# Streaming-encoder trunk on one core: first output sums inside the last input block, regrouped pairs, a fixed load order

## The chip, the core and the metric

One core of a Trainium2 chip runs the whole kernel. The metric is the device time of one execution in microseconds; the time before is 2336.9 us, the median of three runs (2333.71 to 2339.33). The engines are called as in the profile: PE (matrix products) with PEld (its weight loads), DVE (VectorE), ACT (ScalarE), POOL (GpSimd) and SP (SyncE, which here only issues loads).

## The reference, cut to what matters

```python
for i in range(2):
    hn = rmsnorm(h, norm_mix_g[i])
    mix = s5_mixer(hn, ...) if i == 0 else shortconv_mixer(hn, conv_w_in, conv_w, conv_w_out)
    h = h + mix
    gate, up = split(rmsnorm(h, norm_ffn_g[i]) @ ffn_w_in[i])      # 1024 -> 2 x 2816
    h = h + (silu(gate) * up) @ ffn_w_out[i]                       # 2816 -> 1024
    g = sigmoid(rmsnorm(h, norm_ple_g[i]) @ ple_w_gate[i])
    h = h + g * (p[i] @ ple_w_up[i])
return rmsnorm(h, final_norm_g)
# short convolution: b, c, v = split(u @ w_in); y = (b * conv3(c * v)) @ w_out
```

Everything is float32; the sequence has 1024 positions and the model 1024 channels.

## The kernel before, in words

**Precision.** A float32 product is made of three products of a narrower form: each operand is split into a high part (an ACT cast, L90) and a low part (a DVE subtraction, L91), and `mm3` (L123 to L126) adds high x high, high x low and low x high into one PSUM bank. `unit_of` (L118) splits a loaded raw tile into such a pair.

**Tiling.** The 1024 positions are eight row tiles of 128 (`T` = 8, `HT` = 4); tile q and tile q+4 go together as a step q. The big products use a seven-product scheme for 2 x 2 blocks (Strassen's, in a form with few sums), so that for each pair of blocks seven products and a number of sums stand in place of eight products.

**FFN input** (`ffn_in`, L441). 22 blocks, j and j+11 in turn. For each, `weights_set` (L310) loads two raw tiles, makes four sums on DVE and seven split operands in the ring `ws`; `block_product` (L340) makes seven products of 12 matmuls, each 512 wide, with ACT and DVE combining the results. The seven moving operands of a block lie in `ulow` (four of them, quarters `L0` to `L15`, sixteen) and `uhigh` (three, quarters `H0` to `H11`). The hidden units go to DRAM in seven combinations for each j (`hidden[j]`, tile `hw`), by POOL's queue (L456), five stores behind the second block of each j.

**FFN output** (`ffn_out`, L486). The 11 hidden pairs are taken in six groups, two pairs each but the last, which has one. For each group and each of the four steps q: seven products, each of three matmuls a pair, added to rows of h by DVE (`add`, L579) or by an ACT copy and a POOL add (`add_slow`, L586). The operands of a pair come from two raw weight tiles: four subtractions (L508, L512, L517, L520) and seven units, each in a quarter (`make`, L494). Rooms alternate: an even group has the first fourteen low quarters in a list, an odd one the twelve high ones and the last two low ones. The units of the first group are made at the head of `ffn_out` (`run_all(begun)`, L562), those of a later group at the end of the steps of the group before (L621). In the last group each step normalises its two tiles for the gate product (`post`, L609 and L618; `norm_tile`, L193) and the gate's first operands are made (`following`, L623, L625).

**Gate product** (`ple`, L641): for two halves of the columns, eight tiles of 24 matmuls, operands in rooms of `uhigh` and the four tiles `s8t`, which in `ffn_out` hold the chunks of hidden units.

**Convolution** (`conv_in`, `conv_out`). `conv_in` uses the same block product; `conv_out` calls `out_phase` (L382): two groups of four 128-row units, and for each of the eight tiles a chunk of the hidden tensor (`ch`, L403) and, in the first group, the row h of the tile (L406).

**Order.** A planner orders each engine's instructions ahead of time from the order of the program, its own costs and due times; `first()` moves an instruction up by 100 places. Within an engine that order is then fixed. `tc.issue_after(x)` puts what it encloses behind x on x's engine. In `ffn_out` all loads go through `queue` (L532), which chains each SP load behind the one before; `out_phase` only puts the load of h behind the chunk of the same tile. Raw tiles take four slots in turn (`raw_tile`, L95). A pool's memory is reused tile by tile: a load into a new tile waits for the last use of what lay there.

**Between the stages.** `last_pairs` (L251) turns the last rows into the moving operands while the first block already runs, through `others` (L229); the first weight set is loaded early, the second (`weights_set` without `early`) in the ordinary way.

Of the kernel before, what the change touches and what calls it, by code (L numbers as in the profile page):

```python
# [24 lines left out]
def trunk(  # L25
# [225 lines left out]
    def last_pairs(xs, gb):  # L251


        a, z = HT - 2, HT - 1
        with tc.issue_after(done["sum"]), tc.issue_after(done["square"]):
            p = {(0, 0): transposed(xs[a], 0), (1, 0): transposed(xs[a + HT], 0), (1, 1): transposed(xs[a + HT], 1),
                 (0, 1): transposed(xs[a], 1, mm)}
            put(0, a, p[0, 0])
            xs[z], xs[T - 1] = normed(z, gb, 2), normed(T - 1, gb, 2)
            r = {(0, i): transposed(xs[z], i, mm) for i in range(2)}  # L260
            put(0, z, r[0, 0])
            others(a, p)
            n = len(tc.nc.cur_bb.bb.instructions)
            r.update({(1, i): transposed(xs[T - 1], i) for i in range(2)})
            held[:] = [i for i in tc.nc.cur_bb.bb.instructions[n:] if i.engine == PE.engine]
            others(z, r)

# [42 lines left out]
    def weights_set(src_a, src_b):  # L310


        ra, rb = early.pop() if early else [load_raw(src, "p (kt n) -> p kt n", kt=KT) for src in (src_a, src_b)]
        a11, a12, a21, a22 = ra[:, 0:512], ra[:, 512:D], rb[:, 0:512], rb[:, 512:D]

        def operand(src):
            w = wsp.tile([P, 2, 512], F32R, name="ws", tag="ws")
            split(w[:, 0], w[:, 1], src)
            return w

        def s_tile():
            return stp.tile([P, 512], F32, name="st", tag="st")

        w11 = operand(a11)
        s3 = s_tile()
        V.tensor_tensor(s3, a11, a21, ALU.subtract)
        V.tensor_tensor(a21, a21, a22, ALU.add)
        s2 = s_tile()
        V.tensor_tensor(s2, a21, a11, ALU.subtract)
        ws2 = operand(s2)  # L330
        ws1 = operand(a21)
        w12 = operand(a12)
        ws3 = operand(s3)
        V.tensor_tensor(s2, a12, s2, ALU.subtract)
        return [w11, ws2, ws1, w12, ws3, operand(s2), operand(a22)]
# [4 lines left out]
    def block_product(ws, on_c11=None):  # L340


        def prod(ps, i, start):
            for kt in range(KH):
                sl = slice(kt * P, (kt + 1) * P)
                mm3(ps, ws[i][:, 0, sl], ws[i][:, 1, sl], moving(i, kt, 0), moving(i, kt, 1),
                    start and kt == 0, kt == KH - 1, more=not start)

# [33 lines left out]
    def out_phase(wout, groups, last_post, following=(), hold=True):  # L382


        def fetch(ht, room):
            return unit_of(room(), load_raw(wout[ht], "p n -> p n"))

        units = {ht: fetch(ht, room) for ht, room, _ in groups[0]}
        kept = []
        for gi, group in enumerate(groups):  # L390
# [5 lines left out]
            for t in ORDER:  # L396
                parts = {}
                for ht, *_ in group:
                    if ht // 4 not in parts:
                        parts[ht // 4] = ch = raw_tile(shape=(P, 4, 2, P), dt=F32R, name="ch")  # L400
                        of = [x[0] % 4 for x in group if x[0] // 4 == ht // 4]
                        ks = slice(min(of), max(of) + 1)
                        load = nc.sync.dma_start(out=ch[:, ks].bitcast(F32), in_=hid[ht // 4][t, :, ks])  # L403
                if gi == 0:
                    with tc.issue_after(load.ins):
                        nc.sync.dma_start(out=h[t], in_=hdram[t])  # L406
# [34 lines left out]
    def ffn_in(l):  # L441
# [7 lines left out]
        def product(ht):  # L449
            ws = weights_set(win[:, :, ht * P:(ht + 1) * P], win[:, :, HID + ht * P:HID + (ht + 1) * P])  # L450
            return block_product(ws, silu)
# [33 lines left out]

    def ffn_out(l, post, following):  # L486
        wout = ffn_w_out[l].rearrange("(ht p) n -> ht p n", p=P)
        lows = [quarter_low(i) for i in (0, 4, 8, 12, 1, 5, 9, 13, 2, 6, 10, 14, 3, 7, 11, 15)]
        highs = [quarter_high(i) for i in range(12)]
        groups = [list(range(g, min(g + 2, NK))) for g in range(0, NK, 2)]  # L490
        rooms = [lows[:14] if g % 2 == 0 else highs + lows[14:] for g in range(len(groups))]
        combo = {1: 0, 2: 2, 3: 5, 4: 6, 5: 3, 6: 4, 7: 1}

        def make(j, room, got):  # L494
            ra, rb = (raw_tile() for _ in range(2))
            for raw, i in ((ra, j), (rb, j + NK)):
                queue(raw, wout[i])
            if j in groups[0]:
                yield
            b11, b12, b21, b22 = ra[:, 0:512], ra[:, 512:D], rb[:, 0:512], rb[:, 512:D]  # L500

            def unit(i, src):
                v = room.pop(0).rearrange("p (l n) -> p l n", l=2)
                got[i] = unit_of((v[:, 0], v[:, 1]), src)

            unit(1, b11)
            yield
            V.tensor_tensor(b12, b12, b11, ALU.subtract)  # L508
            unit(5, b12)
            yield  # L510
            unit(3, b22)
            V.tensor_tensor(b22, b22, b12, ALU.subtract)  # L512
            unit(6, b22)
            yield
            unit(2, b21)
            yield
            V.tensor_tensor(b11, b22, b11, ALU.subtract)  # L517
            unit(7, b11)
            yield
            V.tensor_tensor(b21, b21, b22, ALU.subtract)  # L520
            unit(4, b21)

        def run_all(gens):
            gens = list(gens)
            while gens:
                for g in list(gens):
                    if next(g, gens) is gens:
                        gens.remove(g)

        queued = []  # L530

        def queue(to, src):  # L532
            with tc.issue_after(queued.pop()) if queued else ExitStack():
                queued.append(nc.sync.dma_start(out=to, in_=src).ins)

# [19 lines left out]
        units = {j: {} for j in range(NK)}  # L555
        begun = []
        for j in groups[0]:
            fetch(0, 0, [j])
            begun.append(make(j, rooms[0], units[j]))
            next(begun[-1])  # L560
        rows(0)
        run_all(begun)  # L562
        pending = []
        for gi, group in enumerate(groups):
            last = gi == len(groups) - 1
            todo = [] if last else [make(j, rooms[gi + 1], units[j]) for j in groups[gi + 1]]
            for q in range(HT):
# [34 lines left out]
                prod(a, 6, False)  # L602
                soft(a, 0, 1)
# [5 lines left out]
                if last:  # L609
                    post(q)  # L610
                prod(a, 7, False)
                add(a, 1, 1, True)

                def finish(a=a, prod=prod, add=add, last=last, q=q):
                    prod(a, 4, False)
                    add(a, 1, 0, True)
                    if last:
# [5 lines left out]
                elif last and following and q > 0:  # L623
                    following.pop(0)()
                if gi == len(groups) - 2 and q > 1:  # L625
                    following.pop(0)()
# [14 lines left out]
    def ple(l, units, post, ahead):  # L641
        more, makers = ple_units(l, 1, [room_new(i) for i in (1, 2, 3, 0)])
        for nb in range(2):
# [5 lines left out]
            for t in ORDER:  # L649
# [16 lines left out]
                if nb == 0 and len(makers) > 2:  # L666
# [647 lines left out]
    def ffn_ple(l, last, ahead):  # L1314
        units, makers = ple_units(l, 0, [room_high(4), room_high(5), room_new(3), room_new(0)])
# [53 lines left out]
```

## Time and profile before

| | us |
|---|---|
| median of three runs | 2336.9 |
| profiled execution, its own time | 2336.83 |
| its span | 2335.1 |
| last FFN input block of layer 0, on PE | 824.2 to 843.2 |
| FFN output of layer 0 | 847.0 to 1091.9 |
| convolution's output, PE | 1437.5 to 1546.0 |
| FFN output of layer 1 | 1987.2 to 2233.5 |

The page gives busy time by engine, the chain that ended last and the costliest groups. A busy time by stretch counts the instructions that touch the stretch, with the granted TensorE clock behind them. In the timeline, a bracket at the end of a line is the idle time of the engine just before that instruction and what ended it. `SPq` and `POOLq` are lines of a sequencer that issues loads or stores.

### The profile page before, as it was taken

To read this page: it belongs to the slowest core of one execution; us is meant where nothing else is said; L and a number is where in the kernel's file an instruction comes from. 1 tells how busy PE (TensorE), PEld (TensorE's weight loads), DVE (VectorE), ACT (ScalarE), POOL (GpSimd) and SP (SyncE) were. 2 spreads that over 40 slices of the span, in tenths; PEclk is the share of its full clock that TensorE was granted. 3 is DMA by queue.
4 is the path that set the end of the run, shared out by engine and by line. 5 is a ranking of instruction groups with operands and counts; after the bars stand their busy time and mean duration, and the time that the engine had idled before them with its cause. 6 is when DMAs were issued, how large, how long until landed. Compare 5 with 4: busy or idle time off the path is not lost.

```text
span 2335.1 us, 27847 instructions
## 1 busy us (share of the span) xinstructions
PE 2189.7 (94%) x9989; PEld 1793.4 (77%) x9989; DVE 1641.1 (70%) x2760; ACT 899.4 (39%) x1717; POOL 350.8 (15%) x426
## 2 busy tenths in 40 slices
PE   7888999899999989999979999979999999799998
PEld 5777887788888867777858887768888888677777
DVE  7885326877777768677587776387777776877674
ACT  6554223444343433234343333154444443333242
POOL 2110001011111113332010000011111111223310
PEclk8999999899999989999989999989999999899999
DMA  8555202344444466672232324433544445775613
GB/s 247 145 137 154 64 19 80 101 144 157 141 153 145 154 256 259 242 275 95 95 104 81 107 92 144 180 127 125 172 145 154 150 154 183 267 259 220 245 55 109
DMA packets 234010, 358.14 MB, mean 153 GB/s; under 512 B 23696, under 2 KB 166032, under 8 KB 233872
## 3 DMA queue, kind: packets, MB, share of 16 engines
q1 hardware_dynamic: 203040, 247.24, 32.2%
q0 software_dynamic: 30432, 109.08, 13.6%
q8 instruction: 79, 1.29, 0.2%
q14 instruction: 59, 0.48, 0.1%
q10 hardware_dynamic: 400, 0.04, 0.0%
HBM read 225.53 MB, written 114.29 MB: 146 GB/s over the span
## 4 chain that ended last, share of the span: by engine, by line
PE 38%; issue 35%; DVE 13%; DMA 7%; POOL 5%; SPq 1%; ACT 1%; POOLq 0%; DVEq 0%; ACTq 0%
PE psmm L124 12%; PE psmm L125 12%; PE psmm L126 12%; POOL hw L456 5%; DVE h L582 2%; DMA raw<-in_ffn_w_out_dram 2%; DVE ulow L91 2%; DMA tw<-tmp 1%; DVE uhigh L91 1%; DVE gv L1160 1%; DVE W L810 1%; DMA h<-hd 1%; DVE tmp L810 1%; DMA hw<-hs 1%; DVE raw L512 1%
## 5 line engine op out<-in xcount | busy, mean ns | idle before, releaser
L124 PE MATMUL psmm<-ulow,ws 128*128 128x512 f32 x896 | 353.4, 396 | 16.3 <-ACT ulow L90 13.8
L125 PE MATMUL psmm<-ulow,ws 128*128 128x512 f32 x896 | 352.7, 394 | 2.5 <-DVE ulow L91 2.5
L126 PE MATMUL psmm<-ulow,ws 128*128 128x512 f32 x896 | 352.1, 393 | 2.0 <-DVE ws L91 2.0
L124 PE MATMUL psmm<-uhigh,ws 128*128 128x512 f32 x672 | 261.8, 390 | 1.8 <-DVE u L361 1.1
L126 PE MATMUL psmm<-uhigh,ws 128*128 128x512 f32 x672 | 261.5, 389 | 0.0
L125 PE MATMUL psmm<-uhigh,ws 128*128 128x512 f32 x672 | 261.4, 389 | 0.0
L456 POOL DMA_DIRECT2D hw<-hs x154 | 116.0, 754 | 792.4 <-DVE hs L91 764.7
L582 DVE TENSOR_TENSOR h<-psmm,h 128x512 f32<-128x512 f32 x244 | 163.5, 683 | 100.4 <-PE psmm L126 57.1
L90 ACT CAST ws<-raw 128x512 fp32r<-128x512 f32 x224 | 138.3, 621 | 193.8 <-PE psmm L126 181.7
L124 PEld LDWEIGHTS psmm<-ulow,ws 128*128 128x128 f32 x896 | 170.9, 191 | 53.1 <-ACT ulow L90 14.7
L125 PEld LDWEIGHTS psmm<-ulow,ws 128*128 128x128 f32 x896 | 170.6, 190 | 39.3 <-DVE ulow L91 3.5
L126 PEld LDWEIGHTS psmm<-ulow,ws 128*128 128x128 f32 x896 | 170.5, 190 | 38.7 <-DVE ws L91 3.0
L591 POOL TENSOR_TENSOR h<-part,h 128x512 f32<-128x512 f32 x92 | 138.6, 1507 | 295.0 <-ACT part L590 225.1
L124 PE MATMUL psmm<-ulow,w 128*128 128x512 f32 x368 | 150.6, 409 | 26.6 <-DVE h L582 12.5
L91 DVE TENSOR_TENSOR ws<-raw,ws 128x512 fp32r<-128x512 f32 x224 | 152.9, 685 | 10.2 <-ACT ws L90 10.1
L125 PE MATMUL psmm<-ulow,w 128*128 128x512 f32 x368 | 148.7, 404 | 6.2 <-DVE ulow L91 6.2
L90 ACT CAST ws<-st 128x512 fp32r<-128x512 f32 x168 | 103.7, 618 | 117.7 <-PE psmm L126 107.6
L124 PEld LDWEIGHTS psmm<-uhigh,ws 128*128 128x128 f32 x672 | 126.2, 188 | 29.2 <-DVE s L369 1.5
L126 PE MATMUL psmm<-ulow,w 128*128 128x512 f32 x368 | 147.8, 402 | 0.0
L126 PEld LDWEIGHTS psmm<-uhigh,ws 128*128 128x128 f32 x672 | 126.1, 188 | 26.2
L125 PEld LDWEIGHTS psmm<-uhigh,ws 128*128 128x128 f32 x672 | 126.2, 188 | 26.1
L125 PE MATMUL psmm<-w,ulow 128*128 128x512 f32 (+1 forms) x328 | 126.2, 385 | 0.0
(267 smaller groups left out, 4442.5 us busy)
## 6 DMA issues: line engine op xcount, KB each, us to landing
hw<-hs POOLq DMA_DIRECT2D x154, 512.0 KB, 4.2
w<-hw SPq DMA_DIRECT2D x88, 768.0 KB, 5.9
raw<-in_ffn_w_in_dram SPq DMA_DIRECT2D x88, 512.0 KB, 4.0
raw<-in_ffn_w_out_dram SPq DMA_DIRECT2D x44, 512.0 KB, 7.6
hd<-h POOLq DMA_DIRECT2D x24, 512.0 KB, 3.0
h<-hd SPq DMA_DIRECT2D x24, 512.0 KB, 7.4
raw<-in_conv_w_in_dram SPq DMA_DIRECT2D x24, 512.0 KB, 3.8
w<-hw SPq DMA_DIRECT2D x88, 128.0 KB, 5.8
```

The costliest lines, as they stand in the source:

```text
L90: A.copy(hi, src)
L91: V.tensor_tensor(lo, src, hi.bitcast(F32), ALU.subtract)
L124: PE.matmul(ps, ahi, bhi, start=start, stop=False, skip_group_check=more)
L125: PE.matmul(ps, ahi, blo, start=False, stop=False, skip_group_check=more)
L126: PE.matmul(ps, alo, bhi, start=False, stop=stop, skip_group_check=more)
L456: nc.gpsimd.dma_start(out=hidden[j][:, :, c].rearrange("q p l j -> p q l j"), in_=hs.bitcast(F32))
L512: V.tensor_tensor(b22, b22, b12, ALU.subtract)
L582: done["sum"] = V.tensor_tensor(h[t][:, cs], ps, h[t][:, cs], ALU.add).ins
L591: G.tensor_tensor(h[t][:, cs], part, h[t][:, cs], ALU.add)
L810: V.tensor_tensor(o, a, b, op)
L1160: V.tensor_tensor_scan(gv[:, g, 1:P], dec, sv[:, g, 1:P], 0.0, ALU.mult, ALU.add)
```

## The change

The diff has six parts.

1. `ffn_out`'s first two pairs are begun inside the last input block: `begin` issues the four weight loads, `block_product` calls `beside(i)` behind product i, and that takes so many steps of the two makers (two each behind the products 0 and 2, one behind 3, three behind 4). The second pair's subtractions go to POOL.
2. The groups are 2, 2, 2, 1, 2, 2 pairs; each pair has a written-out list of quarters; pairs 6 and 7 are made in the third group, 8 in the fourth.
3. In the last group the tiles 2 and 6 are normalised in the last step, and the gate's makers are called two, one, none and one in its steps; the gate's rooms move by one. In a single pair's step the add to the lower right block goes the slow way.
4. `last_pairs` notes the last ACT instruction of its parts, and the second weight set's first operand is issued behind it on ACT.
5. `out_phase` chains its loads: chunk, then row, one tile ahead in the first group, and the later units' weights in the same chain.
6. `make`, `run_all` and `queue` move out of `ffn_out` unchanged but for the above.

```diff
@@ last_pairs
             others(z, r)
+            done["others"] = next(i for i in reversed(tc.nc.cur_bb.bb.instructions) if i.engine == A.engine)
@@ weights_set
+        second = not early and done.pop("others", None)
         ra, rb = early.pop() if early else [load_raw(src, "p (kt n) -> p kt n", kt=KT) for src in (src_a, src_b)]
...
-        w11 = operand(a11)
+        with tc.issue_after(second) if second else ExitStack():
+            w11 = operand(a11)
@@ block_product
-    def block_product(ws, on_c11=None):
+    def block_product(ws, on_c11=None, beside=None):
...
+            if beside:
+                beside(i)
@@ out_phase
-            return unit_of(room(), load_raw(wout[ht], "p n -> p n"))
+            raw = raw_tile()
+            if queued:
+                queue(raw, wout[ht])
+            else:
+                nc.sync.dma_start(out=raw, in_=wout[ht])
+            return unit_of(room(), raw)
+
+        queued.clear()
...
+            def chunk(t, gi=gi, group=group):
+                j = group[0][0] // 4
+                assert [x[0] for x in group] == list(range(4 * j, 4 * j + 4))
+                ch = raw_tile(shape=(P, 4, 2, P), dt=F32R, name="ch")
+                queue(ch.bitcast(F32), hid[j][t])
                 if gi == 0:
-                    with tc.issue_after(load.ins):
-                        nc.sync.dma_start(out=h[t], in_=hdram[t])
+                    queue(h[t], hdram[t])
+                return {j: ch}
+
+            if gi == 0:
+                coming = chunk(ORDER[0])
+            for n, t in enumerate(ORDER):
+                if gi:
+                    parts = chunk(t)
+                else:
+                    parts, coming = coming, None if t == ORDER[-1] else chunk(ORDER[n + 1])
@@ ffn_in
-            return block_product(ws, silu)
+            return block_product(ws, silu, begin(l) if ht == NHT - 1 else None)
@@ ahead of ffn_out
+    groups = [[0, 1], [2, 3], [4, 5], [6], [7, 8], [9, 10]]
+    ROOMS = ["L0 L8 L1 L13 L6 L3 H1", "L4 L12 L5 L2 L10 H0 H2", "L7 L9 L11 L14 L15 H3 H4", "H5 H6 H7 H8 H9 H10 H11",
+             "L0 L8 L1 L13 L6 L3 H1", "L4 L12 L5 L2 L10 H0 H2", "L9 L11 L14 L15 H3 H4 H5", "L7 H6 H7 H8 H9 H10 H11",
+             "L0 L1 L2 L3 L4 L5 L6", "L8 L10 L12 L13 H0 H1 H2", "L9 L11 L14 L15 H3 H4 H5"]
+    MADE = (1, 5, 3, 6, 2, 7, 4)
...
+    def make(l, j, got, eng=None):
+        eng = eng or V
...
+        for raw, i in ((ra, j), (rb, j + NK)):
+            queue(raw, wout[i])
+        yield
...
+        unit(1, b11)
+        yield
+        eng.tensor_tensor(b12, b12, b11, ALU.subtract)
+        unit(5, b12)
+        yield
...
+    def begin(l):
+        units.clear()
+        units.update({j: {} for j in range(NK)})
+        queued.clear()
+        gens = [make(l, j, units[j], G if j else V) for j in groups[0]]
+        for g in gens:
+            next(g)
+        steps = {0: (0, 1, 0, 1), 2: (0, 1, 0, 1), 3: (0,), 4: (1, 0, 1)}
+
+        def beside(i):
+            for g in steps.get(i, ()):
+                next(gens[g], None)
+        return beside
@@ ffn_out
-        groups = [list(range(g, min(g + 2, NK))) for g in range(0, NK, 2)]
-        rooms = [lows[:14] if g % 2 == 0 else highs + lows[14:] for g in range(len(groups))]
...
-        for j in groups[0]:
-            fetch(0, 0, [j])
-            begun.append(make(j, rooms[0], units[j]))
-            next(begun[-1])
+        fetch(0, 0)
         rows(0)
-        run_all(begun)
...
-            todo = [] if last else [make(j, rooms[gi + 1], units[j]) for j in groups[gi + 1]]
+            todo = {2: [6, 7], 3: [8]}.get(gi, [] if last else groups[gi + 1])
+            todo = [make(l, j, units[j]) for j in todo]
...
                 prod(a, 6, False)
+                if last and q == HT - 1:
+                    post(HT - 2)
+                    post(T - 2)
...
-                if last:
+                if last and q != HT - 2:
                     post(q)
                 prod(a, 7, False)
-                add(a, 1, 1, True)
+                if len(group) == 1:
+                    add_slow(a, 1, 1)
+                else:
+                    add(a, 1, 1, True)
...
-                    if last:
+                    if last and q != HT - 2:
                         post(q + HT)
...
-                elif last and following and q > 0:
-                    following.pop(0)()
-                if gi == len(groups) - 2 and q > 1:
-                    following.pop(0)()
+                if last:
+                    for _ in range((2, 1, 0, 1)[q]):
+                        following.pop(0)()
@@ ple
-        more, makers = ple_units(l, 1, [room_new(i) for i in (1, 2, 3, 0)])
+        more, makers = ple_units(l, 1, [room_new(i) for i in range(4)])
...
-                if nb == 0 and len(makers) > 2:
+                if nb == 0 and len(makers) > 1:
                     makers.pop(0)()
@@ ffn_ple
-        units, makers = ple_units(l, 0, [room_high(4), room_high(5), room_new(3), room_new(0)])
+        units, makers = ple_units(l, 0, [room_high(3), room_high(4), room_high(5), room_new(3)])
```

More of the change, by code (lines that the diff above doesn't have):

```diff
@@ L395, in out_phase @@
             soon, late = [f for early, f in todo if early], [f for early, f in todo if not early]
[L396 to L403, printed above, removed]
-                if gi == 0:
-                    with tc.issue_after(load.ins):
-                        nc.sync.dma_start(out=h[t], in_=hdram[t])
+            def chunk(t, gi=gi, group=group):
[3 more added lines that the diff above has]
+                queue(ch.bitcast(F32), hid[j][t])
+                if gi == 0:
+                    queue(h[t], hdram[t])
[7 more added lines that the diff above has]
+                    parts, coming = coming, None if t == ORDER[-1] else chunk(ORDER[n + 1])
                 ps = [psum() for _ in range(2)]
@@ L484, in quarter_high @@
         return uhigh.rearrange("p c k l j -> p (c k l j)")[:, i * D:(i + 1) * D]
-    def ffn_out(l, post, following):
-        wout = ffn_w_out[l].rearrange("(ht p) n -> ht p n", p=P)
-        lows = [quarter_low(i) for i in (0, 4, 8, 12, 1, 5, 9, 13, 2, 6, 10, 14, 3, 7, 11, 15)]
-        highs = [quarter_high(i) for i in range(12)]
-        groups = [list(range(g, min(g + 2, NK))) for g in range(0, NK, 2)]
-        rooms = [lows[:14] if g % 2 == 0 else highs + lows[14:] for g in range(len(groups))]
-        combo = {1: 0, 2: 2, 3: 5, 4: 6, 5: 3, 6: 4, 7: 1}
[L494 to L534, printed above, removed]
@@ new lines, in trunk, with queue @@
+    groups = [[0, 1], [2, 3], [4, 5], [6], [7, 8], [9, 10]]
[3 more added lines that the diff above has]
+    MADE = (1, 5, 3, 6, 2, 7, 4)
+    queued = []
+    def queue(to, src):
+        with tc.issue_after(queued.pop()) if queued else ExitStack():
+            queued.append(nc.sync.dma_start(out=to, in_=src).ins)
@@ new lines, in run_all, with unit @@
+    def run_all(gens):
+        gens = list(gens)
+        while gens:
+            for g in list(gens):
+                if next(g, gens) is gens:
+                    gens.remove(g)
+    def make(l, j, got, eng=None):
+        eng = eng or V
+        wout = ffn_w_out[l].rearrange("(ht p) n -> ht p n", p=P)
+        rooms = {i: (quarter_low if r[0] == "L" else quarter_high)(int(r[1:])) for i, r in zip(MADE, ROOMS[j].split())}
+        ra, rb = (raw_tile() for _ in range(2))
+        for raw, i in ((ra, j), (rb, j + NK)):
+            queue(raw, wout[i])
+        yield
+        b11, b12, b21, b22 = ra[:, 0:512], ra[:, 512:D], rb[:, 0:512], rb[:, 512:D]
+        def unit(i, src):
+            v = rooms[i].rearrange("p (l n) -> p l n", l=2)
+            got[i] = unit_of((v[:, 0], v[:, 1]), src)
+        unit(1, b11)
[3 more added lines that the diff above has]
+        yield
+        unit(3, b22)
+        eng.tensor_tensor(b22, b22, b12, ALU.subtract)
+        unit(6, b22)
+        yield
+        unit(2, b21)
+        yield
+        eng.tensor_tensor(b11, b22, b11, ALU.subtract)
+        unit(7, b11)
+        yield
+        eng.tensor_tensor(b21, b21, b22, ALU.subtract)
+        unit(4, b21)
@@ new lines, in trunk @@
+    units = {}
+    def begin(l):
[10 more added lines that the diff above has]
+        return beside
+    def ffn_out(l, post, following):
+        combo = {1: 0, 2: 2, 3: 5, 4: 6, 5: 3, 6: 4, 7: 1}
@@ L554, in ffn_out @@
         steps = [(gi, q) for gi in range(len(groups)) for q in range(HT)]
-        units = {j: {} for j in range(NK)}
-        begun = []
-        for j in groups[0]:
-            fetch(0, 0, [j])
-            begun.append(make(j, rooms[0], units[j]))
-            next(begun[-1])
+        fetch(0, 0)
         rows(0)
-        run_all(begun)
         pending = []
```

## The prediction

> **What bounds the kernel now.** I read the page first, then busy times by stretch of the matmul engine, then its waits, then the timeline of the stretches that lose time.
>
> ```profile
> span 2335.1 us, 27847 instructions
> ## 1 busy us (share of the span) xinstructions
> PE 2189.7 (94%) x9989; PEld 1793.4 (77%) x9989; DVE 1641.1 (70%) x2760; ACT 899.4 (39%) x1717; POOL 350.8 (15%) x426
> ```
>
> PE is the bound, so a change can win only what PE loses. The profiled execution took 2336.83 us, 1.7 more than its span, and the median of the runs is 2336.9; the sum is made against 2336.8 and stands for the median too.
>
> Busy time by stretch, all engines: one whole block of the FFN's input (the last of layer 0), then a piece of what follows it. The columns are PE, PEld, DVE, ACT, POOL with their counts, granted clock, DMA share, GB/s.
>
> ```profile
> 824.25:843.25 19.00, 18.98 (x84) 15.39 (x82) 7.29 (x11) 3.62 (x6) 1.50 (x2) 1.00 0.79 296
> 845.00:850.00 5.00, 1.25 (x2) 0.74 (x3) 4.88 (x9) 2.77 (x6) 2.84 (x4) 0.66 1.02 402
> ```
>
> 84 matmuls in 19.00 us is 0.226 us for a 512-wide one when nothing is in the way. In this block DVE is free for 19.00 - 7.29 = 11.7 us and ACT for 15.4, because no next weights are prepared; straight after it DVE is full and PE starves. The same view for PE alone, at the places that the change touches:
>
> ```profile
> 843.25:866.90 23.65, 12.11 (x27) 0.71 0.78 305
> 870.60:1061.80 191.20, 184.79 (x799) 1.00 0.69 254
> 1059.30:1091.80 32.50, 26.85 (x120) 0.95 0.26 89
> 1457.50:1467.90 10.40, 3.72 (x9) 0.67 0.94 364
> 1983.50:2007.20 23.70, 12.34 (x27) 0.71 0.79 300
> 2010.85:2203.80 192.95, 185.97 (x799) 0.99 0.68 252
> 2201.40:2233.45 32.05, 26.94 (x116) 0.89 0.25 91
> ```
>
> Start of the FFN's output, both layers: 27 matmuls are worth 27 x 0.226 = 6.1 us but took 23.65 and 23.70, so 17.5 us are lost each time, part of them because the granted clock is 0.71. The groups behind it lose 191.20 - 798 x 0.226 = 10.8 us and 12.6 (one of the 799 reaches over the edge), spread thinly. The last group: 84 matmuls (19.0 us) and 36 or 32 transposes; at 0.11 us for a transpose (the row of eight below) that is 23.0 and 22.5 against 32.50 and 32.05: 9.5 us lost each. The convolution's output: 10.40 - 9 x 0.226 = 8.4 us lost.
>
> ```profile
> 1089.60 1.03 PE L204 MATMUL pstr<-ident,xn 128*128 128x128 f32 x8
> ```
>
> What ended PE's waits:
>
> ```profile
> PE psmm L124 <- ACT ulow L90: 23.9, 7, 6.0
> PE psmm L124 <- DVE h L582: 22.5, 22, 3.4
> ```
>
> L90 on ulow is mostly the making of the first operands of the FFN's output; L582 is the adding of products to h.
>
> **Part 1: the first sums inside the last input block.** Timeline, PE, then ACT and DVE:
>
> ```profile
> 846.98 0.80 PE L124 MATMUL psmm<-ulow,w 128*128 128x512 f32 x1 [3.76 <-ACT ulow L90]
> ...
> 863.38 0.61 PE L124 MATMUL psmm<-ulow,w 128*128 128x512 f32 x1 [3.39 <-DVE h L582]
> ```
>
> ```profile
> 848.92 1.66 ACT L90 CAST ulow<-raw 128x512 fp32r<-128x512 f32 x3 [1.99 <-DVE raw L508]
> ```
>
> ```profile
> 860.24 1.89 DVE L91 TENSOR_TENSOR ulow<-raw,ulow 128x512 fp32r<-128x512 f32 x3
> 862.04 0.68 DVE L91 TENSOR_TENSOR hs<-s,hs 128x512 fp32r<-128x512 f32 x1
> 862.64 0.68 DVE L582 TENSOR_TENSOR h<-psmm,h 128x512 f32<-128x512 f32 x1
> ```
>
> After the block DVE makes 14 operands and 8 subtractions, 22 operations, and only behind them comes the first add to h (862.64), for which PE waits a second time. In a row a DVE operation costs (1.89 - 0.68)/2 = 0.605 us and an ACT cast (1.66 - 0.62)/2 = 0.52. The change moves all of it under the block's products: 14 casts = 7.3 us in ACT's 15.4 free, and on DVE 14 + 4 = 18 operations = 10.9 us in its 11.7 free; four subtractions of the second pair go to POOL, which has 17.5 free. So it just fits, and the 17.5 us go, if the weights are there:
>
> ```profile
> 828.02 0.90 SPq L534 DMA_DIRECT2D raw<-in_ffn_w_out_dram  x2
> 832.38 1.49 SPq L534 DMA_DIRECT2D w<-hw  x2
> 833.98 0.94 SPq L534 DMA_DIRECT2D raw<-in_ffn_w_out_dram  x2
> 834.97 1.26 SPq L534 DMA_DIRECT2D h<-hd  x2
> 837.82 6.24 SPq L534 DMA_DIRECT2D w<-hw  x4
> 848.35 3.09 SPq L534 DMA_DIRECT2D h<-hd  x2
> ```
>
> The second pair's weights were issued behind a hidden-unit load that waited for room until 832.38. Now the four weight loads are first in the chain and wait only for the raw slots of the last two weight sets, which are read before the block starts; they should go by about 822. The hidden loads that they pass are held by their own rooms, so they lose nothing.
>
> What is late next: (a) the block's closing work, about 8 DVE operations after its last product (4.9 us), against a first add due one product (6 x 0.226 = 1.4 us) in. PE can do one more product, so the add costs between 0 (it goes first) and 4.9 + 0.6 - 2.7 = 2.8 us; I take 2.5, since the closing work is older in the plan. (b) The rows of h for the second step:
>
> ```profile
> h<-hd SPq DMA_DIRECT2D x8, 512.0 KB, 7.8
> ```
>
> Issued at 848.35 and 851, they land at about 859. Without loss the second step starts at 843.25 + 42 x 0.226 = 852.7, its third product ends at 856.8, PE does one more to 858.2 and then needs that add, done at 859.6: 1.4 us. (c) Bytes: a step of the first group now loads two hidden sets of 917,504 bytes (the shape in the code), two rows of h and two weight rows of 524,288 each, 3.93 MB. At the 402 GB/s of the row above that is 9.8 us against a step of 9.5: 0.3 x 3 steps = 0.9 us. The Trainium skill ("DMA: Bandwidth & Descriptors", Where 436 GB/s comes from) puts a core's share of HBM at about 358 GB/s; by it a step takes 11.0 us and the three steps lose 3.6 us more in each layer; the row of 402 speaks against it. Left over: 2.5 + 1.4 + 0.9, say 5 us of 17.5. Gain 12.5 a layer, **25 us**; ends 6 and 17.
>
> **Part 2: the single pair moves from the last group to the fourth.** In the last group each step has two tiles to normalise, and a single pair's step gives PE only 21 x 0.226 + 16 x 0.11 = 6.5 us:
>
> ```profile
> L201 DVE SCALAR_TENSOR_TENSOR xn<-h,rs,gb x32: 739/746/1778, 1069.4 to 2258.4; 128x512 f32<-128x512 f32 x32
> ```
>
> DVE needs five adds (3.0) and for each tile two such scalings (median 0.746) and two splits (0.605), 2 x 2.7 = 5.4: 8.4 us with nothing going wrong, and more than 6.5. With a double pair PE has 42 x 0.226 + 1.8 = 11.3 us, so DVE is covered. I keep 3 us for the last step, where four tiles pile up (they run on under the gate products that follow, which need tile 2 only four tiles later). The single pair now meets the slow adds:
>
> ```profile
> L591 POOL TENSOR_TENSOR h<-part,h x92: 1263/1294/2942, 872.8 to 2243.8; 128x512 f32<-128x512 f32 x92
> ```
>
> Three per step (one more than before) are 3.9 us on POOL against 4.75 of PE; two adds of DVE wait for POOL, so I book 0.6 a step, 2.4 us. Gain 9.5 - 3 - 2.4 = 4, **8 us** for two layers; ends -9 and 9.5 a layer, since the median alone hides POOL's 2.9. The rooms with names change no operation. The gate's first units are made two a step earlier, the fourth in the last step behind a chunk's room; the cover is the first tile's six quarters (18 x 0.226 = 4 us), and without it one load (7.8 us, above) and a cast and a split of twice the width (some 2 us) would show.
>
> **Part 3: the second weight set's first cast behind the last transposed parts.** ACT:
>
> ```profile
> 420.49 0.62 ACT L90 CAST ws<-raw 128x512 fp32r<-128x512 f32 x1 [1.82 <-DMA raw<-in_ffn_w_in_dram]
> ```
>
> ```profile
> 1213.89 0.62 ACT L90 CAST ws<-raw 128x512 fp32r<-128x512 f32 x1 [2.65 <-DMA raw<-in_conv_w_in_dram]
> ```
>
> ACT sits waiting for a load with the casts that PE waits for behind it (the 6.0 of the waits is this place in layer 1). Held back, the cast lets them pass: at most 1.82 + 0.52 and 2.65 + 0.52, 5.5 together, at least 0 if DVE's splits come next; **4 us**. Behind the held cast stand only casts for a block that starts some 15 us later.
>
> **Part 4: fixed load order in the convolution's output.**
>
> ```profile
> 1453.98 4.73 SPq L403 DMA_DIRECT2D ch<-hid  x2
> 1458.76 2.62 SPq L406 DMA_DIRECT2D h<-hd  x5
> ```
>
> ```profile
> 1463.43 0.69 DVE L418 TENSOR_TENSOR h<-psmm,h 128x512 f32<-128x512 f32 x1 [2.98 <-DMA h<-hd]
> ```
>
> Five h rows stand on SP behind a chunk that waits for its slot until 1458, so the first add is at 1463 and PE stops with full banks. Chained, the first row follows the first chunk. Of 8.4 us I take **8**, at least 3 if the next chunk is late instead.
>
> **Sum:** 25 + 8 + 4 + 8 = 45; 2336.8 - 45 = 2292.
>
> **Rivals.** *The covers are too thin* (20%): beside a POOL add a scaling took up to 1778 ns where 746 is the median, so a collision costs DVE 1.0 us. Four POOL subtractions a layer add 4 us to 10.9 of 11.7, and the loads of the group add the rest of 6.5: part 1 gives 6 a layer, in all 12 + 8 + 4 + 8 = 32: 2305. The Trainium skill ("SBUF — State Buffer", Who interferes with whom) says that a DVE instruction with two SBUF inputs and a GpSimd one that reads SBUF lock each other out; by it each collision costs up to the other's whole length, which 1778 against 746 bears out. *The single pair backfires* (9%): POOL's adds at 2.9 us, three a step, make it 8.8 instead of 4.75, 4 x 4 = 16 us lost, -9 a layer after the 9.5 won: 25 - 18 + 4 + 8 = 19: 2318. *It isn't done as said* (9%): the planner orders ACT and DVE by its own due times and may keep the sums behind the block's stores, as it does now with weights that had been issued at 828: part 1 gives nothing, 20 us: 2317. *Slower* (6%): the chain in part 4 turns on itself: each load waits for the one ahead and that for a slot freed at a tile's end, as the chunk of 1453.98 already did for 4 us. If all eight tiles of the first round waited one landing of 7.8 us, that is 62 us: 2336.8 - 37 + 62 - 8.4 = 2353. It decides from (37 + 8.4)/8 = 5.7 us a tile. Against it: a tile's chunk is queued a whole tile (24 x 0.226 = 5.4 us) ahead.
>
> **Numbers.** Forecast 52% (2292, its own spread 2272 to 2303), rivals 20, 9, 9 and 6%, 4% that gains and losses cancel. A measurement of this kernel can tell about 0.2%, 4.7 us. Faster 0.52 + 0.20 + 0.09 + 0.09 = 0.90, same 0.04, slower 0.06. The low end is nearly all of parts 1 and 2 won (34 + 19 + 4 + 8); the high end takes in all the rivals but the slower one: 2272 to 2318.
>
> **What would show it.** Part 1: no wait of PE over 3 us at the start of the FFN's output, L90/L91 on ulow inside the block, granted clock near 1.00 there; wrong if these casts stand behind the stores, or if PE waits inside the block. Part 2: last group without waits on L582, the fourth under 22 us for 84 matmuls. Part 3: the wait on ulow near 417 and 1210 shorter by 2. Part 4: h rows issued before 1440, no wait on L418. The prediction is wrong if the time is over 2318, above all if PE loses in the first group what it wins ahead of it.

## The result, and the profile after

The changed kernel takes 2297.05 us (median of four runs, 2295.53 to 2300.29) against 2338.11 for the kernel before on the same chip. The ratio of the runs is 0.9828, 95% interval 0.9808 to 0.9848 (the two medians alone give 0.9824). The forecast was 2292 in a range of 2272 to 2318. The time is inside the range and close to the forecast, but two terms of the sum are wrong in opposite directions, as the places show. First the page of the changed kernel:

```profile
span 2293.3 us, 27860 instructions
PE 2169.0 (95%) x9989; PEld 1785.8 (78%) x9989; DVE 1632.9 (71%) x2744; ACT 902.5 (39%) x1725; POOL 368.7 (16%) x442
```

The span is 41.8 us shorter with the same 9989 matmuls. Of the two waits that the prediction quoted, one fell and one grew:

```profile
PE psmm L124 <- DVE h L611: 28.1, 16, 8.9
PE psmm L124 <- ACT ulow L90: 9.8, 3, 3.6
```

The wait for operands (L90) went from 23.9 us to 9.8. The wait for sums of h (L582 before, now L611) went from 22.5 to 28.1, and its longest from 3.4 to 8.9: a wait has taken the place of the one removed. Busy time of PE by stretch, changed kernel: the first steps of the FFN's output in both layers, the group of the single pair, the last group, and the convolution's output (length, busy and matmuls, granted clock, DMA share, GB/s):

```profile
842.10:862.70 20.60, 11.68 (x43) 0.75 0.85 300
1958.00:1978.80 20.80, 11.85 (x44) 0.75 0.83 296
970.80:994.35 23.55, 20.27 (x85) 1.00 0.56 195
2090.15:2111.05 20.90, 19.70 (x85) 1.00 0.64 220
1033.90:1070.50 36.60, 36.52 (x177) 1.00 0.51 183
2150.50:2189.00 38.50, 37.21 (x177) 1.00 0.52 182
1437.20:1447.60 10.40, 10.16 (x46) 1.00 0.81 284
```

At the first steps 43 matmuls are worth 43 x 0.226 = 9.7 us and took 20.60: 10.9 us are lost, in layer 1 also 10.9, where 17.5 were lost before and 5 were forecast. In the last group, where 9.5 were lost, PE is idle for 0.1 in layer 0 and 1.3 in layer 1. The convolution's output loses next to nothing. By the starts of the same PE instructions in the two traces, what each place gave (minus: lost):

| place | layer 0, us | layer 1, us |
|---|---|---|
| last operands before the FFN input, first block (part 3) | 3.4 | 0.5 |
| convolution's output (part 4) | | 9.0 |
| rest of the FFN's input, to its last block's end | -2.4 | -3.1 |
| first group of the FFN's output (part 1) | 7.8 | 8.2 |
| second to fifth group | -0.7 | -1.4 |
| last group and what follows it (part 2) | 11.1 | 9.9 |

Together 42.3 us, against 41.8 between the spans. Part 1 is the first group less the 1.9 us that its work now costs inside the last input block (below): 16.0 - 3.8 = 12 us against the 25 forecast. Part 2 is 21.0 less the 2.1 that the groups before it lose, 19 against 8.

Where part 1 went: PE in the changed kernel, inside the block and behind it.

```profile
839.24 0.50 PE L124 MATMUL psmm<-uhigh,ws 128*128 128x512 f32 x1 [1.90 <-DVE s L374]
...
855.26 0.80 PE L124 MATMUL psmm<-ulow,w 128*128 128x512 f32 x1 [8.92 <-DVE h L611]
855.86 0.63 PE L125 MATMUL psmm<-ulow,w 128*128 128x512 f32 x1
856.28 0.63 PE L126 MATMUL psmm<-ulow,w 128*128 128x512 f32 x1
...
859.27 0.40 PE L124 MATMUL psmm<-ulow,w 128*128 128x512 f32 x1
```

PE makes three products and then waits 8.92 us for the first add. The first nine matmuls behind the wait (855.26 to 859.27) take 4.0 us, worth 2.0 at full rate; 8.92 + 2.0 is the 10.9 lost. ACT and DVE at that place:

```profile
853.27 0.62 ACT L90 CAST hs<-s 128x512 fp32r<-128x512 f32 x1 [7.16 <-DMA hw<-hs]
```

```profile
853.92 0.69 DVE L91 TENSOR_TENSOR hs<-s,hs 128x512 fp32r<-128x512 f32 x1 [6.11 <-ACT hs L90]
854.53 2.08 DVE L611 TENSOR_TENSOR h<-psmm,h 128x512 f32<-128x512 f32 x3
```

Read from the end: three adds stand behind DVE's split of the fifth, last hidden store. That split waits for ACT's cast, and the cast waits 7.16 us for a DMA: the ring `hs` has four buffers, the block stores five times in quick succession, and the fifth needs a buffer whose store has landed. The stores of this stretch take longer than the 4.2 us of the page's row:

```profile
hw<-hs POOLq DMA_DIRECT2D x5, 512.0 KB, 6.1
```

In the kernel before, the fifth store's split is the row of 862.04 that the prediction shows, with the first add right behind it at 862.64. It had no wait of its own there, with 19 us of operand making ahead of it. At other places the same ring did make ACT wait in the kernel before, and the list of its waits said so (us in all, times, longest):

```profile
ACT hs L90 <- DMA hw<-hs: 67.3, 18, 6.8
```

In layer 0 nine of these 18 waits stand before the fifth stores of nine of the eleven pairs, 2.58 to 6.80 us each. They cost PE nearly nothing there, because the products of the next block ran meanwhile: in the stretches of ten to twelve us around them PE is busy for 97.28 of 98.00 us. At the last block what runs meanwhile is the FFN's output, which needs DVE's adds.

Inside the block POOL's subtractions meet DVE's splits. POOL, then DVE:

```profile
827.97 1.60 POOL L541 TENSOR_TENSOR raw<-raw 128x512 f32<-128x512 f32 x1 [10.77 <-DVE ulow L91]
...
831.19 1.31 POOL L546 TENSOR_TENSOR raw<-raw 128x512 f32<-128x512 f32 x1
```

```profile
828.34 1.78 DVE L91 TENSOR_TENSOR hs<-s,hs 128x512 fp32r<-128x512 f32 x1
830.04 0.68 DVE L541 TENSOR_TENSOR raw<-raw 128x512 f32<-128x512 f32 x1
830.65 3.01 DVE L91 TENSOR_TENSOR ulow<-raw,ulow 128x512 fp32r<-128x512 f32 x2
```

A split takes 0.68 alone; the one beside the subtraction of 827.97 takes 1.78, and two, the first of them (2.41) beside the subtraction of 831.19, take 3.01 where 0.68 + 0.605 is usual. DVE falls behind, and PE waits 1.90 for a combination (L374) that stands in its queue.

### The profile page after: what moved, and what is told of

It is laid out like the page before. It is cut to its first block, busy times and chain, and to the rows that moved or that the text cites. A ratio compares the mean times of both kernels' runs of the same rounds, so it can differ in the third digit from the quotient of the medians.

```text
span 2293.3 us, 27860 instructions
## 1 busy us (share of the span) xinstructions
PE 2169.0 (95%) x9989; PEld 1785.8 (78%) x9989; DVE 1632.9 (71%) x2744; ACT 902.5 (39%) x1725; POOL 368.7 (16%) x442
## 4 chain that ended last, share of the span: by engine, by line
PE 63%; issue 14%; DVE 13%; DMA 6%; POOL 2%; ACT 1%; SPq 1%; DVEq 0%; POOLq 0%; ACTq 0%
PE psmm L124 20%; PE psmm L126 20%; PE psmm L125 20%; DVE h L611 2%; DMA raw<-in_ffn_w_out_dram 2%; DVE ulow L91 2%; POOL hw L473 2%; DVE uhigh L91 1%; DMA tw<-tmp 1%; DMA w<-hw 1%; DMA hw<-hs 1%; DVE W L844 1%; DVE gv L1194 1%; DVE tmp L844 1%; PE pstr L204 1%
## 5 line engine op out<-in xcount | busy, mean ns | idle before, releaser
L611 DVE TENSOR_TENSOR h<-psmm,h 128x512 f32<-128x512 f32 x236 | 157.7, 684 | 76.6 <-PE psmm L126 42.0
L90 ACT CAST ws<-raw 128x512 fp32r<-128x512 f32 x224 | 138.4, 621 | 174.8 <-PE psmm L126 166.8
L620 POOL TENSOR_TENSOR h<-part,h 128x512 f32<-128x512 f32 x100 | 145.8, 1462 | 261.7 <-ACT part L619 220.2
L90 ACT CAST ws<-st 128x512 fp32r<-128x512 f32 x168 | 103.8, 618 | 122.2 <-PE psmm L126 111.8
L91 DVE TENSOR_TENSOR ws<-st,ws 128x512 fp32r<-128x512 f32 x168 | 116.0, 691 | 16.0 <-ACT ws L90 15.8
```

Of the source, the lines that this page charges most:

```text
L90: A.copy(hi, src)
L91: V.tensor_tensor(lo, src, hi.bitcast(F32), ALU.subtract)
L611: done["sum"] = V.tensor_tensor(h[t][:, cs], ps, h[t][:, cs], ALU.add).ins
L620: G.tensor_tensor(h[t][:, cs], part, h[t][:, cs], ALU.add)
```

## The experiments

Each edit is made to the changed kernel, unless another base is named. Ratios are to the kernel before, with their 95% intervals; the changed kernel's is 0.9828. The kernel before was run again beside the experiments (medians 2335.74 to 2337.64), the changed kernel was not, so a difference from its 2297.05 us is uncertain by some 5 us. The theory was: part 1 is held up by the last store's room and by POOL's subtractions, and part 2 gave more than forecast. The rivals were that part 2 gave little and part 1 nearly all, and that the first add is late for another reason (rows of h, bytes, the split itself).

### Each part taken back

Part 1 undone, the sums made at the head of the FFN's output:

```diff
-            return block_product(ws, silu, begin(l) if ht == NHT - 1 else None)
+            return block_product(ws, silu)
@@ ffn_out
-        fetch(0, 0)
...
+        begun = []
+        for j in groups[0]:
+            fetch(0, 0, [j])
+            begun.append(make(l, j, units[j]))
+            next(begun[-1])
         rows(0)
+        run_all(begun)
```

> Part 1 alone undone: the first two pairs' sums and splits are made at the head of the FFN's output again, all subtractions on DVE. Theory A (one store buffer short: in the changed kernel the adds of the first step stand on DVE behind the split of the block's last hidden store, whose cast waits for a store to land): part 1 gave only about 6 us a layer, so 2309 +- 3, and the wait of PE on the first casts is back. The prediction's own price, 12.5 a layer: 2322.

Measured: 2305.19 us, ratio 0.9865 (0.9851 to 0.9878), 8.1 us above the changed kernel and a little under what the theory expected. PE's waits at the head of layer 0's FFN output in this kernel are those of the kernel before again:

```profile
PE psmm L124 <- ACT ulow L90: 5.4, 2, 3.8
PE psmm L124 <- DVE h L619: 3.5, 1, 3.5
PE psmm L125 <- DVE ulow L91: 3.1, 2, 1.8
```

Twelve microseconds of waits in five pieces were exchanged for 8.92 in one and 1.90 in the block. By its undoing part 1 is worth 8 us, by the table above 12, and not 25.

Part 2 undone, the single pair last again:

```diff
-    groups = [[0, 1], [2, 3], [4, 5], [6], [7, 8], [9, 10]]
+    groups = [[0, 1], [2, 3], [4, 5], [6, 7], [8, 9], [10]]
@@ ffn_out
-            todo = {2: [6, 7], 3: [8]}.get(gi, [] if last else groups[gi + 1])
+            todo = [] if last else groups[gi + 1]
...
-                if last and q == HT - 1:
-                    post(HT - 2)
-                    post(T - 2)
...
-                if last and q != HT - 2:
+                if last:
                     post(q)
```

(with the lists of quarters, the gate's makers and its rooms set to suit, and no third `add_slow`.)

> Part 2 alone undone: groups of 2, 2, 2, 2, 2, 1 pairs, every last step normalises its own two tiles, rooms to match. Reading of the two traces (last group lost 9.5 a layer and now loses nothing): about 10 us a layer, 2317 +- 3. The prediction's price, 4 a layer: 2305.

Measured: 2313.86 us, 0.9902 (0.9889 to 0.9916), 16.8 us above the changed kernel and at the low end of what the reading of the traces expected: part 2 is the largest part. The last group of layer 0 in this kernel, PE by stretch and what ended its waits:

```profile
1049.30:1081.80 32.50, 24.02 (x110) 1.00 0.28 101
```

```profile
PE psmm L124 <- DVE h L611: 4.4, 6, 0.9
PE pstr L204 <- DVE xn L201: 3.2, 4, 1.5
```

8.5 of 32.50 us are idle, nearly all in these ten small waits for DVE. In the changed kernel the same normalising, beside two pairs instead of one, leaves PE idle for 0.08 of 36.60.

Parts 3 and 4 undone:

```diff
-        with tc.issue_after(second) if second else ExitStack():
-            w11 = operand(a11)
+        w11 = operand(a11)
```

> Part 3 alone undone: the second weight set's first operand is no longer held behind the last transposed parts on ACT. The traces show PE's waits there shorter by 1.8 and 2.5, so 2301 +- 2 (the prediction's 4). Rival: nothing that can be measured, 2297, if the splits on DVE set that start anyway.

Measured: 2299.88 us, 0.9847 (0.9834 to 0.9861). The time alone does not tell it from the changed kernel; the waits at the place do. Without the hold, near 415 us, and with it (changed kernel):

```profile
PE psmm L124 <- ACT ulow L90: 5.3, 1, 5.3
```

```profile
PE psmm L124 <- ACT ulow L90: 2.9, 1, 2.9
```

In layer 1 the two are 5.2 and 3.6. Part 3 is worth 2.4 + 1.6 = 4 us of waits. The median moved by 2.8. By the starts of PE's instructions the two traces differ by 2.2 at the place in layer 0 and by nothing in layer 1, so that the shorter wait won time in layer 1 is not shown.

```diff
-                queue(ch.bitcast(F32), hid[j][t])
                 if gi == 0:
-                    queue(h[t], hdram[t])
+                    with tc.issue_after(load.ins):
+                        nc.sync.dma_start(out=h[t], in_=hdram[t])
```

(the chunk and the unit loads as before the change too.)

> Part 4 alone undone: the convolution's output loads its chunks, rows and units in the planner's order. By the traces and by the prediction PE again waits some 7 us on the first add of that stage: 2305 +- 2. Rival (the rows come early enough once the rest has moved): 2297.

Measured: 2304.83 us, 0.9864 (0.9850 to 0.9877), 7.8 us above the changed kernel. The wait is back, at the place of before (the convolution's output, this kernel):

```profile
PE psmm L124 <- DVE h L423: 6.1, 1, 6.1
```

In the changed kernel the rows of h go out one tile ahead, each behind its chunk, and nothing waits for them. Two of its loads:

```profile
1434.32 0.32 SPq L512 DMA_DIRECT2D ch<-hid  x1
1434.69 0.42 SPq L512 DMA_DIRECT2D h<-hd  x1
```

The four prices are 8.1 + 16.8 + 2.8 + 7.8 = 35.5 of about 41. With each uncertain by some 5 us the rest asks for no further cause, but it does not exclude one.

### What holds part 1 up

The fifth store gets a room of its own, a raw slot:

```diff
-            hs = hsp.tile([P, HT, 2, P], F32R, name="hs", tag="hs")
+            if j == NK - 1 and c == 5:
+                hs = raw_tile(shape=(P, HT, 2, P), dt=F32R, name="hs")
+            else:
+                hs = hsp.tile([P, HT, 2, P], F32R, name="hs", tag="hs")
```

> Changed kernel, but the last hidden store of a layer takes a raw slot in place of a buffer of the ring of four, so its cast need not wait for an earlier store to land. Theory A: PE's wait of 8.9 at the FFN output's start falls to about 3, 5 to 7 us a layer: 2284 to 2288. Rival B (the loads set that start: rows of h and weights at the full DMA rate): the wait moves into the second step, 2293 to 2297.

Measured: 2283.51 us, 0.9773 (0.9759 to 0.9786), 13.5 us below the changed kernel, at the low end of what theory A expected. PE and DVE in this kernel:

```profile
848.77 0.50 PE L124 MATMUL psmm<-ulow,w 128*128 128x512 f32 x1 [3.55 <-DVE h L614]
```

```profile
847.42 0.69 DVE L91 TENSOR_TENSOR hs<-s,hs 128x512 fp32r<-128x512 f32 x1 [0.74 <-ACT hs L90]
848.03 2.08 DVE L614 TENSOR_TENSOR h<-psmm,h 128x512 f32<-128x512 f32 x3
```

The 8.92 became 3.55: 5.4 us in each layer, 10.8 of the 13.5. The rest of the wait is the closing work itself, with the adds still behind the last split; the prediction had put exactly this term at 0 to 2.8 us. Rows of h and bytes are not what the first add waited for.

The second pair's subtractions go back from POOL to DVE:

```diff
-        eng = eng or V
+        eng = V
```

> Changed kernel with the second pair's four subtractions on DVE instead of POOL. Theory C (POOL and DVE block each other: splits of up to 2.4 us beside POOL's subtractions, and PE's wait of 1.9 in the block): without POOL the splits are 0.68 again, the 1.9 goes, 4 x 0.6 us of own work come: 2293 to 2297. If POOL's help is worth what it was meant for: 2298 to 2302, with PE waiting more inside the block.

Measured: 2288.30 us, 0.9793 (0.9780 to 0.9807), 8.8 us below the changed kernel, with four more operations a layer on DVE, and 5 us below the nearer end of what theory C expected. DVE's splits in 821 to 840 us, the changed kernel and then this one (the last number before the bar's end is the mean in ns):

```profile
L91 DVE TENSOR_TENSOR ulow<-raw,ulow 128x512 fp32r<-128x512 f32 x11 | 8.8, 840 | 0.3 <-PE psmm L126 0.3
```

```profile
L91 DVE TENSOR_TENSOR ulow<-raw,ulow 128x512 fp32r<-128x512 f32 x9 | 5.9, 688 | 0.0
```

The wait inside the block fell from 1.9 to 0.2, and the FFN output starts 2.3 us earlier in each layer. That is 4.6 of the 8.8 us; where the other 4 come from the traces do not say, and single groups differ by 1 to 3 us from trace to trace. The 8.7 us wait for the last store stays, so the two causes are separate.

Both together:

> Changed kernel with both repairs: the last hidden store in a raw slot, and all subtractions on DVE. If the two losses are separate, as theories A and C have it (one inside the block, one behind it), they add: 2297 - 13 - 8 = 2276 +- 3. If they are the same loss seen twice (DVE late by so much at the block's end), the better of the two alone: 2283.

Measured: 2276.69 us, 0.9746 (0.9732 to 0.9760). The two gains add up (13.5 + 8.8 = 22.3 expected from 2297.05, 20.4 measured). This version beats both kernels, 59 us below the kernel before beside it and 20 below the change, and is called the best version from here on. Its first steps of the FFN output in both layers:

```profile
840.40:861.00 20.60, 17.05 (x68) 0.92 0.96 347
1948.80:1969.60 20.80, 17.25 (x69) 0.92 0.96 346
```

68 matmuls are worth 15.4 us and took 20.60: 5.2 us are lost, where the prediction's left-over was 5. The sizes agree, the contents do not: here it is 3.55 of the wait for the first add and some 1.6 of lower clock behind it.

### Attempts at the rest

The first add made the slow way, an ACT copy and a POOL add, on top of the best version, so that it need not stand in DVE's queue:

```diff
-                soft = add_slow if gi or q else add
+                soft = add_slow
```

> As e7_room_and_dve, and in the very first step the upper left and upper right blocks go the slow way (ACT copy, POOL add) as in all other steps, so that PE's bank is freed without DVE. If what is left of the wait at the start (3.5) is the block's closing work on DVE ahead of the first add, it falls below 1.5 and 2 to 3 us a layer go: 2270 to 2273. If PE is held there by the products' operands or by the loads: no gain, 2274 to 2278.

Measured: 2283.21 us, 0.9776 (0.9763 to 0.9789): 6.5 us worse than without, and outside both expectations. PE and ACT in this kernel:

```profile
845.79 0.50 PE L124 MATMUL psmm<-ulow,w 128*128 128x512 f32 x1 [3.62 <-ACT part L622]
...
848.34 0.80 PE L124 MATMUL psmm<-ulow,w 128*128 128x512 f32 x1 [0.67 <-ACT part L622]
```

```profile
845.15 0.58 ACT L622 COPY part<-psmm 128x512 f32<-128x512 f32 x1 [0.81 <-DVE hs L91]
```

The copy is released by the same split of the last store (844.37 to 845.06 on DVE), so it comes no earlier; which room or order ties the two was not tried. PE waits as long as before, then a second time, and behind that the granted clock is 0.59 over 8.3 us (845.70 to 854.00), where the best version has 0.75 over 6.8 (848.20 to 855.00).

The single pair's third slow add, put back on DVE (best version as the base):

```diff
-                if len(group) == 1:
-                    add_slow(a, 1, 1)
-                else:
-                    add(a, 1, 1, True)
+                add(a, 1, 1, True)
```

> The best version so far (last store in a raw slot, subtractions on DVE, 2276.7) with the third slow add of a single pair's step put back on DVE: two POOL adds a step in place of three, four adds on DVE in place of three. If the single pair's step loses time because of POOL's adds (the reading behind the prediction's 2.4 us a layer: POOL's adds take 1.29 alone, but x3 took 5.12 us in the fourth group of the changed kernel), the fourth groups lose less: 4 to 5 us off, 2272. If DVE is what is full there (seven operands, four subtractions and the adds within 4.75 us a step), 0.6 us more on DVE for each of 8 steps costs up to 4.8 us: 2281. If neither, 2276.7.

Measured: 2278.59 us, 0.9750 (0.9737 to 0.9763): no difference from the best version that the time can tell. And, on top of that edit, all of a single pair's adds on DVE:

```diff
-                soft = add_slow if gi or q else add
+                soft = add_slow if len(group) > 1 and (gi or q) else add
```

> The same with all of a single pair's adds on DVE: no POOL add in the fourth group at all, six adds on DVE a step. If POOL's collisions are the loss, no collision is left there: DVE has 6 x 0.6 = 3.6 us of adds and about 2.75 operands and subtractions a step (11 in four steps) x 0.6 = 1.7, 5.3 us against 4.75 of PE, so at best 2272 and, by the excess of 0.55 us in each of 8 steps, 2277 to 2281. If DVE is what is full, 2286 (1.8 us a step more than in the version with three slow adds, less what slack it has).

Measured: 2279.76 us, 0.9752 (0.9739 to 0.9765): no difference either. The fourth group of layer 0, PE in the best version (three slow adds a step) and then in the version with none:

```profile
966.75:987.60 20.85, 19.65 (x85) 1.00 0.62 221
```

```profile
967.20:989.20 22.00, 20.16 (x85) 1.00 0.62 209
```

And DVE's splits in 960 to 990 us of the same two:

```profile
L91 DVE TENSOR_TENSOR ulow<-raw,ulow 128x512 fp32r<-128x512 f32 x7 | 6.3, 921 | 0.0
```

```profile
L91 DVE TENSOR_TENSOR ulow<-raw,ulow 128x512 fp32r<-128x512 f32 x7 | 4.6, 687 | 0.0
```

Without POOL's adds no split is stretched, but DVE has three more adds a step, and the group is 1.1 us longer; with two slow adds it takes 22.00 as well. One cost replaces the other, and the single pair's third slow add is worth about that 1.1 us a layer. So the readings that put 4 us or more on the third slow add, for or against it, fell, and the version with none lies where POOL's collisions and DVE's own excess together were expected to put it (2277 to 2281).

## Why the prediction came out as it did, point by point

**The bound.** Right: PE is busy for 95% of the span and every microsecond won is one that PE had lost at a named place.

**Part 1** is the step that failed, and in it the item "What is late next: (a)". It counted the closing work as DVE operations, 0 to 2.8 us, took 2.5, and gave a left-over of 5 in all. It took the last of those operations to be ready when DVE gets to it. The runs put 8.92 in its place, and 2.0 more for the matmuls at half rate behind the wait, for which the sum had no term: DVE works through its instructions in a fixed order, the fifth store's split waits for a ring buffer and so for a landing, and the adds stand behind it. With a buffer free the item is 3.55, a little over its upper bound: DVE then has ten operations and a 0.74 us wait for ACT ahead of the first add, and not eight, so that this ends 7.7 us behind the block's last product, while PE gets three products (4.1 us) further and not two. The profile of before had what was needed to ask about the ring: its wait of 67.3 us in the list, five stores, the add right behind the last split, and the making ahead of them that the change was about to take away. Two of the prediction's own signs against part 1 came, a wait of PE over 3 us at the start of the FFN's output and a wait inside the block; the granted clock there was 0.75, not near 1.00.

The second piece of the same part, "it just fits" (10.9 us of DVE's 11.7), fell too. The rival of thin covers named the mechanism, a POOL operation that stretches DVE's, and gave part 1 as 6 us a layer; that is what part 1 gave by the table. Of the prediction's two prices for part 1 the rival's was right, with one cause that it named and one that it didn't. Items (b) and (c) were too high: no wait of PE for rows of h shows up, and the waits for `w` in these steps of the best version are 0.6 at most. So the left-over of 5, which the best version meets with 5.2, was right by luck.

**Part 2** was right in its mechanism and wrong in its size: 19 us by place and 16.8 by its undoing, against 8. The mis-sized term is the 3 us kept for four tiles piling up in the last step: the last group lost 0.1 and 1.3, because what is left of the normalising runs under the gate products, as the bracket in the prediction itself says (in layer 0 the scalings go on to 1081.7 us, and the gate products start at 1070.6). The 2.4 a layer booked for the single pair was about right in layer 1 (20.90 - 84 x 0.226 = 1.9). In layer 0 the profiled run shows 4.5 there, and so does the run with the old load order; the other traces with three slow adds have 1.9 at the same place, and what makes the difference is open. The reason given for it, POOL's three adds, is not all of it, since with two of them or none the group loses 3.0. And groups two to five as a whole lose about a microsecond a layer more than before, so the single pair costs less in the middle than was booked.

**Part 3**: 3.4 + 0.5 us by place and 2.8 by its undoing, against 4. **Part 4**: 9.0 by place and 7.8 by its undoing, against 8. In both the waits come back when the edits are taken back. For part 4 and for layer 0 of part 3 the time at the place comes back too; for layer 1 of part 3 it does not.

**The sum** of 45 met 41 by luck in its two largest terms: by place, part 1 fell short by 13 and part 2 exceeded by 11; the rest of the difference lies in the input blocks, spread thinly. The other rivals did not come: the single pair did not turn on the middle groups, the sums do lie inside the block, and the convolution's chain delays nothing.

## What to carry to other kernels

When work is taken out from ahead of a step, list what then stands directly in front of that step on its in-order engine, and for each of those instructions every room and load that it needs; a wait for a ring that costs nothing in one place may only be covered there. Count stores against buffers where several are made in a burst. And before work goes to POOL to relieve DVE, compare it with leaving it on DVE: here four subtractions of 0.6 us a layer cost more on POOL than they saved.

## What the runs showed of the hardware

**The clock falls some time after PE has gone idle, even if PE is back at work by then.** PE by stretch: the changed kernel's 8.92 us wait (846.35 to 855.26) and what follows it, then the kernel with the fifth room, behind its 3.55 us waits in layer 0 (ends at 848.77) and in layer 1 (ends at 1961.36):

```profile
846.35:849.00 2.65, 0.00 (x0) 1.00 0.93 311
849.05:855.25 6.20, 0.00 (x0) 0.50 1.00 330
855.25:859.25 4.00, 3.98 (x9) 0.50 1.03 410
```

```profile
850.30:853.65 3.35, 3.35 (x9) 0.50 0.99 356
1961.35:1971.35 10.00, 9.99 (x44) 1.00 1.01 365
```

In the changed kernel the granted clock stays at 1.00 for 2.7 us of the wait, then it is 0.50 for 10.2 us, and the first nine matmuls behind the wait still go 0.43 us apart instead of 0.23: 2.0 us more on top of the wait. Behind the 3.55 us wait of layer 0 the matmuls run at full rate for 1.5 us and then at half rate for 3.4; behind the same wait in layer 1 no fall shows, and none behind the 1.90 us wait of the changed kernel. The Trainium skill ("TensorE: Matmul & The Clock Gate", What's actually happening) describes a free-running activity window of about 3.4 us, half rate after an idle one and full rate after a busy one. Stretches of 3.4 and of three times 3.4 us at half rate fit that, and so does a fall that comes early, late or not at all behind waits of one length. In the best version the 3.55 us wait was followed by a fall in both layers and cost 1.6 us beyond itself (5.2 lost in its row above).

**A POOL operation stretches a DVE one beside it.** DVE's splits took 687 to 691 ns on average in the versions without POOL work at the place, 840 to 1128 with it, and 1.78 us in a row above; POOL's two subtractions in the rows above took 1.60 and 1.31. The Trainium skill ("SBUF — State Buffer", Who interferes with whom) says that the two lock each other out; the stretched splits agree. Taking the eight subtractions off POOL made the kernel 8.8 us faster, of which 4.6 is traced to these collisions in the block.

**The transfers of this one core ran above the share that the prediction weighed.** In the best version, just behind the restart (PE, PEld, DVE, ACT, POOL, clock, DMA share, GB/s):

```profile
855.00:858.00 3.00, 3.00 (x15) 2.49 (x14) 1.06 (x2) 0.59 (x1) 0.38 (x1) 1.00 1.03 410
```

410 GB/s with PE fully busy is above the 358 of the Trainium skill's page that the prediction cited ("DMA: Bandwidth & Descriptors", Where 436 GB/s comes from), a figure that the page gets by halving a stack's rate between two cores, while one core ran here. PE lost nothing in that stretch, and in these steps no wait of PE for a load is over 0.6 us: the 3.6 us a layer that would follow from 358 did not come.
